# RWKV-7 and GLA trunk on one core: the recurrence's right sides and state update moved to ScalarE and one PSUM bank

## The chip, the core and the metric

The kernel runs on one core of one Trainium2 chip. The time of a run is the device time of that core in microseconds (us). TensorE is called PE, VectorE DVE, ScalarE ACT, GpSimd POOL, and SP is the queue that issues the loads. PSUM is the memory that PE writes to; it has eight banks.

## What is computed

Two layers on 272 tokens of width 2048, each followed by a squared-ReLU MLP. The change concerns the first mixer, RWKV-7, whose core is a recurrence over tokens for each of 32 heads of 64 channels:

```python
def step(S, inp):
    r_t, w_t, k_t, v_t, a_t, b_t = inp
    sa = einsum('bhvk,bhk->bhv', S, a_t)
    S = S * w_t[:, :, None, :] + sa[..., None] * b_t[:, :, None, :] + v_t[..., None] * k_t[:, :, None, :]
    y = einsum('bhvk,bhk->bhv', S, r_t)
    return S, y
...
mu = mean(y); var = mean((y - mu)^2)
y = (y - mu) * rsqrt(var + eps) * ln_w + ln_b
out = ((y + bonus) * g) @ w_o
```

The second mixer (gated linear attention), the two MLPs and the norms are touched by nothing but the names of two PSUM tags.

## The kernel before

All weights are float32. `wload` brings one block of 128x1024 in by DMA, ACT rounds it to `hi` (L134), DVE computes the rest `lo` (L135), and `mm3` forms each product by three matmuls, hi by x-high, hi by x-low, lo by x-high (L140 to L142). `raw` has three buffers and `hi` and `lo` two each, so a block can be rounded only when PE has finished with the block before the last.

**The recurrence in chunks.** The 32 heads are worked off in four groups (g = 0 to 3) of eight heads, the tokens in four chunks (c = 0 to 3) of 64 and one (c = 4) of 16. For a group and chunk these pieces follow each other:

- `centre` (L553) brings the values, less their mean over a head, to the token layout (tile `uv`, copied by ACT, L564). `keys` (L566) transposes the keys (tile `bkt`, one buffer, ACT L571).
- `inner` (L574) multiplies the masked scores `AM` with the values (bank `pm`), and ACT takes the result out negated as the right side `rs` (L581).
- `state` (L584) multiplies `AR` with the state `S` (tile `sb`, 128 x 4 x 64): once into the bank `pu`, which DVE then adds to `rs` (L595, two instructions), and once into `pry`, the output's bank.
- `solve` (L598) multiplies `rs` with the inverted score matrix, and ACT copies the result into `uv` (L607).
- `emit` (L609) first forms the state's increment in `pu` (L616). DVE adds the old state and multiplies with the decays `WC`, two instructions of 128x256 (tile `S`, under L268, the line of the helper `tt`). Then it adds the output products (L624) and ACT copies the output (`yc`, L627).
- `turn` (L629) transposes the output of the chunk before into `hres`; `norm(g)` (L640) is a generator with two steps for each of a group's four feature blocks: a product for the variance (L648, bank `pm`), logarithm and exponential on ACT (L649, L650), then on DVE a scaling and an addition (L652, L268), the gate's products (L657, bank `pm`) and DVE's final product (L658).

**The inversion of the next group.** `scores(g+1, c)` (L407) forms the next group's score matrices (PE L416; DVE masks them: `AM`, `AMr`). When the last of the five stands, `invert(g+1)` (L423) solves all their triangular 32x32 systems side by side on DVE: transposes in (L431, L434), 30 steps of two dependent instructions (`upd`, `sysA`), transposes out (L445, L449). `merge(g+1)` (L523) puts the 32-blocks together: a transpose on DVE (L526) of the short chunk's part from `sysA` into an `rs` buffer, from which ACT copies it (L527), and PE products (L535, L545).

**What sets the order.** PE's order in this part is written out by hand (`manual_schedule`, from L756): beside the recurrence PE works through `products()`, the big projections, one step of three matmuls at a time. `R(n)` runs n steps, `until(n)` runs up to step n, with the counts in `GAPS` and `MARK`. `some(last, n)` runs n steps of the norm of the group before, `some(inv, 9)` writes out nine steps of the inversion. The orders of DVE and ACT are not written by hand: a scheduler decides them when the program is built, and each engine then works its own list strictly from front to back. A `wload` stands in the program at the fourth step of the block before.

Of the kernel before, what the change touches and what calls it, by code (L numbers as in the profile page):

```python
# [12 lines left out]
ALU = mybir.AluOpType  # L13
# [4 lines left out]
P = 128  # L18
# [4 lines left out]
T = NMETA + SEQ  # L23
# [3 lines left out]
HEAD = 64  # L27
# [26 lines left out]
class Kern:  # L54
# [24 lines left out]
        return self.pt("pj", 2)  # L79

    def pm(self):
        return self.pt("pm", 2)

    def ptr(self):
        return self.pt("pt", 2)
# [2 lines left out]
        return self.pt("pry", 1)  # L88

    def pu(self):  # L90
        return self.pt("pu", 1)

    def vec(self, name, j):
        c = VI[name] * KT + j
# [171 lines left out]
    def rwkv(self, done):  # L266
        nc, tc, ap = self.nc, self.tc, self.ap
# [67 lines left out]
        nc.vector.tensor_scalar(out=om0, in0=self.vecs[:, c : c + KT], scalar1=-1.0, scalar2=1.0, op0=ALU.mult,  # L335
                                op1=ALU.add)
        xr = [self.t(self.xp, [P, 2, T], "x", KT, F32R) for _ in range(KT)]
        pss = [f()[:, :T] for f in (self.pj, self.pj, self.ptr, self.ptr, self.pm, self.pm, self.pry, self.pu)]
        for kt in range(KT):
            nc.vector.scalar_tensor_tensor(out=hnp[:, kt, 1:], in0=d[:, kt], scalar=self.vec("norm_mix0", kt),  # L340
                                           in1=rstd, op0=ALU.mult, op1=ALU.mult)
# [22 lines left out]
        def lora(f):  # L364
            l2 = self.t(e2, [96, 2, P], "l2", 2)
            nc.sync.dma_start(l2, ap["lora2"][f])
            st = self.t(ep, [P, 2, T], "ca", 2)
            zw, za = self.pm(), self.pm()
# [83 lines left out]
        for f in range(KT):  # L452
# [26 lines left out]
            rk = self.pm()[:, :T]  # L479
# [32 lines left out]
        uvs, rss, bkts, rys, ys = {}, {}, {}, {}, {}  # L512

        def geom(g, c):
            full = c < NC4
# [57 lines left out]

        def inner(g, c):  # L574
            full, n, nr, am, lo, up, at = geom(g, c)
            uv, rv = uvs[g, c], half(self.pm())
            for h in range(8):
                nc.tensor.matmul(rv[at[h % 2][0], h // 2], am[:n, h, :n], uv[:n, h], start=True, stop=True)
            rs = rss[g, c] = self.t(kp, [P, 512], "rs", 2).rearrange("p (h v) -> p h v", h=8)
            for q in range(2):  # L580
                nc.scalar.mul(rs[up, q::2], rv[at[q][0]], -1.0)  # L581


        def state(g, c):  # L584
            full, n, nr, am, lo, up, at = geom(g, c)
            rs, AR = rss[g, c], ARs[g % 2]
            ry = rys[g, c] = half(self.pry())
            ra = half(self.pu())
            for p in range(4):
                for q, i in ((0, 0), (1, 1), (1, 0), (0, 1)):  # L590
                    rows = slice(64 * q, 64 * q + 64)
                    nc.tensor.matmul((ra, ry)[i][at[q][i], p], AR[rows, p, c * 128 + i * n : c * 128 + (i + 1) * n],
                                     sb[rows, p], start=i == 0 or p == 0, stop=i == 0)
            for q in range(2):
                nc.vector.scalar_tensor_tensor(out=rs[up, q::2], in0=ra[at[q][0]], scalar=-1.0, in1=rs[up, q::2],  # L595
                                               op0=ALU.mult, op1=ALU.add)

        def solve(g, c):  # L598
            full, n, nr, am, lo, up, at = geom(g, c)
            uv, rs, pu = uvs[g, c], rss[g, c], half(self.pu())  # L600
            nu = n if full else 16
            for h in range(8):
                o = n * (1 - h % 2)
                nc.tensor.matmul(pu[o : o + nu, h // 2], am[up, h, :nu], rs[up, h], start=True, stop=True)
            for q in range(2):
                o = n * (1 - q)
                nc.scalar.copy(uv[n : n + nu, q::2], pu[o : o + nu])  # L607

        def emit(g, c):  # L609
            full, n, nr, am, lo, up, at = geom(g, c)  # L610
            uv = uvs[g, c]
            if full:
                pS = half(self.pu())
                for h in range(8):
                    k = slice(64 * (h % 2), 64 * (h % 2) + 64)
                    nc.tensor.matmul(pS[k, h // 2], bkts[g, c][:, h // 2, k], uv[:, h], start=True, stop=True)  # L616
                src = pS
                if c:
                    tt(sb, pS, sb, ALU.add)
                    src = sb  # L620
                tt(sb, src, WC[:, 4 * g : 4 * g + 4, c : c + 1].to_broadcast([P, 4, HEAD]))
            ry = rys[g, c] if c else half(self.pry())
            for h in range(8):
                nc.tensor.matmul(ry[at[h % 2][1], h // 2], am[: 2 * n, h, n : 2 * n], uv[: 2 * n, h],  # L624
                                 start=c == 0 and h < 2, stop=h > 5)
            y = ys[g, c] = self.t(kp, [P, 4, HEAD], "yc", 2)
            nc.scalar.copy(y[: 2 * n], ry[: 2 * n])  # L627
# [120 lines left out]
        def some(it, n):  # L748
            for _ in range(n):
                next(it, None)  # L750
# [5 lines left out]
        with tc.manual_schedule(engines={mybir.EngineType.PE}):  # L756
# [9 lines left out]
            for g in range(NG):  # L766
                more = g + 1 < NG
                for c in range(5):
                    if c:
                        state(g, c)  # L770
                        turn(g, c - 1)
                    if more and c < 2:
                        scores(g + 1, 2 * c)
                    elif not more:
                        some(last, 1)
                    R(GAPS[g][c][0])
                    some(inv, 9)
                    solve(g, c)
                    if c in (1, 3):
                        centre(g, c + 1)  # L780
                    if c < 3:
                        keys(g, c + 1)
                    if more and c < 2:
                        scores(g + 1, 2 * c + 1)
                    some(last, 4)
                    R(GAPS[g][c][1])
                    if more and c == 1:
                        scores(g + 1, 4)
                        inv = invert(g + 1)
                    some(inv, 9)  # L790
                    emit(g, c)
                    if c < 4:
                        inner(g, c + 1)
                    if g + 2 < NG and c == 2:
                        fetch(g + 2, BKs, bkd)
                    if g + 2 < NG and c == 3:
                        fetch(g + 2, ARs, ard, 0, 512)
                    if g + 2 < NG and c == 4:
                        fetch(g + 2, ARs, ard, 512)
# [273 lines left out]
```

## Time and profile before

| | us |
|---|---|
| median of 3 runs | 2653.16 (2652.71 to 2655.34) |
| the profiled execution | 2651.93 |
| its span | 2649.9 |
| PE busy | 2551.9 (96%) |
| DVE busy | 1688.0 (64%) |
| ACT busy | 1257.3 (47%) |

The recurrence lies between about 325 and 665 us of the span. In the view of windows that stretch has PE busy for 291.08 of its 340 us, DVE for 235.25 and ACT for 155.55, at a mean granted PE clock of 0.94; from 700 us on PE is all but never idle. In a timeline a row's bracket tells the idle time of its engine before it and what ended it.

### The profile page before, as it was taken

To read this page: it belongs to the slowest core of one execution; us is meant where nothing else is said; L and a number is where in the kernel's file an instruction comes from. 1 tells how busy PE (TensorE), PEld (TensorE's weight loads), DVE (VectorE), ACT (ScalarE), POOL (GpSimd) and SP (SyncE) were. 2 spreads that over 40 slices of the span, in tenths; PEclk is the share of its full clock that TensorE was granted. 3 is DMA by queue.
4 is the path that set the end of the run, shared out by engine and by line. 5 is a ranking of instruction groups with operands and counts; after the bars stand their busy time and mean duration, and the time that the engine had idled before them with its cause. 6 is when DMAs were issued, how large, how long until landed. Compare 5 with 4: busy or idle time off the path is not lost.

```text
span 2649.9 us, 47706 instructions
## 1 busy us (share of the span) xinstructions
PE 2551.9 (96%) x19492; PEld 2364.2 (89%) x19492; DVE 1688.0 (64%) x2794; ACT 1257.3 (47%) x2011; POOL 10.8 (0%) x35
## 2 busy tenths in 40 slices
PE   7998988888999999999999999999999999999998
PEld 7887977777999999999999999998888888888887
DVE  8677976775755545545545666676766656656665
ACT  5364644445544434434434544454555535435444
POOL 0000000000000000000000000000000000000000
PEclk9998999989999999999999999999999999999999
DMA  5565732322455555555555544444555555555554
GB/s 192 180 217 205 245 137 85 100 79 93 160 174 176 175 175 175 176 176 178 177 177 176 176 150 148 155 167 144 188 186 189 186 189 189 186 189 189 186 190 159
DMA packets 137083, 450.17 MB, mean 170 GB/s; under 512 B 15760, under 2 KB 23696, under 8 KB 136864
## 3 DMA queue, kind: packets, MB, share of 16 engines
q1 hardware_dynamic: 136864, 447.12, 49.3%
q8 instruction: 153, 2.51, 0.4%
q14 instruction: 66, 0.54, 0.1%
HBM read 431.07 MB, written 15.99 MB: 169 GB/s over the span
## 4 chain that ended last, share of the span: by engine, by line
PE 77%; DVE 3%; ACT 1%; issue 0%; DVEq 0%; ACTq 0%
PE pj L168 23%; PE pj L140 13%; PE pj L142 13%; PE pj L141 13%; PE pj L169 12%; DVE lo L135 1%; PE pt L908 1%; PE pm L657 0%; PE pu L917 0%; DVE upd L268 0%; PE pt L897 0%; DVE sysA L268 0%; PE pm L648 0%; PE pm L558 0%; PE pt L416 0%
## 5 line engine op out<-in xcount | busy, mean ns | idle before, releaser
L134 ACT CAST hi<-raw 128x1024 fp32r<-128x1024 f32 (+1 forms) x834 | 813.6, 983 | 1086.7 <-PE pj L141 566.8
L135 DVE TENSOR_TENSOR lo<-raw,hi 128x1024 fp32r<-128x1024 f32 (+1 forms) x834 | 946.8, 1142 | 596.6 <-ACT hi L134 583.6
L140 PE MATMUL pj<-x,hi 128*128 128x272 f32 x2224 | 657.0, 296 | 6.6 <-ACT x L308 4.1
L142 PE MATMUL pj<-x,lo 128*128 128x272 f32 x2224 | 645.1, 290 | 0.2 <-DVE lo L135 0.2
L141 PE MATMUL pj<-x,hi 128*128 128x272 f32 x2224 | 643.4, 289 | 0.0
L168 PE MATMUL pj<-x,hi 128*128 128x512 f32 x1664 | 587.6, 396 | 0.6 <-DVE x L827 0.6
L169 PE MATMUL pj<-x,lo 128*128 128x256 f32 x1664 | 468.6, 282 | 1.3 <-DVE lo L135 1.3
L140 PEld LDWEIGHTS pj<-x,hi 128*128 128x128 f32 x2224 | 421.4, 190 | 15.1 <-ACT x L308 4.9
L141 PEld LDWEIGHTS pj<-x,hi 128*128 128x128 f32 x2224 | 424.2, 191 | 2.0
L142 PEld LDWEIGHTS pj<-x,lo 128*128 128x128 f32 x2224 | 420.7, 189 | 1.6 <-DVE lo L135 0.7
L168 PEld LDWEIGHTS pj<-x,hi 128*128 128x128 f32 x1664 | 313.2, 188 | 76.3 <-issue 2.9
L168 PE MATMUL pj<-h,hi 128*128 128x512 f32 x1024 | 358.5, 394 | 0.0
L169 PEld LDWEIGHTS pj<-x,lo 128*128 128x128 f32 x1664 | 314.1, 189 | 2.8 <-DVE lo L135 1.9
L140 PE MATMUL pj<-h,hi 128*128 128x272 f32 x1024 | 294.7, 288 | 0.0
L142 PE MATMUL pj<-h,lo 128*128 128x272 f32 x1024 | 293.9, 287 | 0.0
L141 PE MATMUL pj<-h,hi 128*128 128x272 f32 x1024 | 293.5, 287 | 0.0
L169 PE MATMUL pj<-h,lo 128*128 128x256 f32 x1024 | 288.5, 282 | 0.0
L168 PEld LDWEIGHTS pj<-h,hi 128*128 128x128 f32 x1024 | 192.4, 188 | 44.3
L141 PEld LDWEIGHTS pj<-h,hi 128*128 128x128 f32 x1024 | 193.7, 189 | 0.0
L169 PEld LDWEIGHTS pj<-h,lo 128*128 128x128 f32 x1024 | 193.5, 189 | 0.0
L140 PEld LDWEIGHTS pj<-h,hi 128*128 128x128 f32 x1024 | 192.6, 188 | 0.0
L142 PEld LDWEIGHTS pj<-h,lo 128*128 128x128 f32 x1024 | 192.1, 188 | 0.0
(246 smaller groups left out, 2223.1 us busy)
## 6 DMA issues: line engine op xcount, KB each, us to landing
raw<-mlp_w_d SPq DMA_DIRECT2D x512, 512.0 KB, 3.2
raw<-gla_in_d SPq DMA_DIRECT2D x98, 512.0 KB, 3.2
raw<-w_rkv_d SPq DMA_DIRECT2D x80, 512.0 KB, 3.7
raw<-gla_o_d SPq DMA_DIRECT2D x32, 512.0 KB, 3.2
raw<-w_r_d SPq DMA_DIRECT2D x16, 512.0 KB, 3.3
raw<-rw_oA_d SPq DMA_DIRECT2D x16, 512.0 KB, 3.3
raw<-rw_oB_d SPq DMA_DIRECT2D x16, 512.0 KB, 3.2
ard<-ar SPq DMA_DIRECT2D x16, 288.0 KB, 3.7
```

Of the source, the lines that this page charges most:

```text
L134: nc.scalar.copy(hi[:, h], raw[:, h])
L135: nc.vector.tensor_tensor(out=lo[:, h], in0=raw[:, h], in1=hi[:, h].bitcast(F32), op=ALU.subtract)
L140: nc.tensor.matmul(out, hi[:, ws], xh, start=first, stop=False)
L141: nc.tensor.matmul(out, hi[:, ws], xl, start=False, stop=False)
L142: nc.tensor.matmul(out, lo[:, ws], xh, start=False, stop=last)
L168: nc.tensor.matmul(wide, hi[:, ws], x[kt][:, :, off : off + SEQ], start=kt == 0, stop=False)
L169: nc.tensor.matmul(ps[:, :SEQ], lo[:, ws], x[kt][:, 0, off : off + SEQ], start=False, stop=kt == nk - 1)
L908: nc.tensor.matmul(pa[:w, i * C : (i + 1) * C], KX[i][:, dt, s * P : s * P + w], Q[:, dt, i * C : (i + 1) * C], start=dt == 0, stop=dt == 1)
```

## The change

- `inner` of the chunk c+1 writes into a `pu` bank and leaves it open; `state` adds its products with `S` into the same bank, so the sum of the right side forms in PSUM. A new function `sides` takes it out negated, two ACT instructions after `state`. DVE's two additions (L595) are gone.
- `carry` puts the old state into a further `pu` bank by four products with the identity matrix (c = 1 to 3). `learn` adds the increment to it there, and ACT writes the state in four instructions of 128x64, each scaled by a column of `WC`. DVE's addition and multiplication are gone.
- PSUM: `pu` has two banks, `pm` one (before one and two). Three other places take another tag for it (`rk`, `za`, one of eight accumulators).
- The hand-written order: `learn`, then `inner` of the next chunk, then `emit`, then `keys` of the next chunk (before: `keys` ahead of the increment, then increment, output, `inner`). The norm of the group before runs in chunks 2 and 3, two steps ahead of each gap; before it ran in chunks 0 and 1, four steps in a row. In the last group it stays where it was.

```diff
     def pm(self):
-        return self.pt("pm", 2)
+        return self.pt("pm", 1)
     def pu(self):
-        return self.pt("pu", 1)
+        return self.pt("pu", 2)
...
         def inner(g, c):
-            uv, rv = uvs[g, c], half(self.pm())
+            uv = uvs[g, c]
+            ra = ras[g, c] = half(self.pu())
             for h in range(8):
-                nc.tensor.matmul(rv[at[h % 2][0], h // 2], am[:n, h, :n], uv[:n, h], start=True, stop=True)
-            rs = rss[g, c] = self.t(kp, [P, 512], "rs", 2).rearrange("p (h v) -> p h v", h=8)
+                nc.tensor.matmul(ra[at[h % 2][0], h // 2], am[:n, h, :n], uv[:n, h], start=h < 2, stop=c == 0 and h > 5)
+            if c == 0:
+                sides(g, c)
+        def sides(g, c):
+            rs = ras[g, c, "rs"] = self.t(kp, [P, 512], "rs", 2).rearrange("p (h v) -> p h v", h=8)
             for q in range(2):
-                nc.scalar.mul(rs[up, q::2], rv[at[q][0]], -1.0)
+                nc.scalar.mul(rs[up, q::2], ras[g, c][at[q][0]], -1.0)
...
         def state(g, c):
-            for q in range(2):
-                nc.vector.scalar_tensor_tensor(out=rs[up, q::2], in0=ra[at[q][0]], scalar=-1.0, in1=rs[up, q::2],
-                                               op0=ALU.mult, op1=ALU.add)
+            sides(g, c)
...
+        def carry(g, c):
+            pS = pSs[g, c] = half(self.pu())
+            if c:
+                for p in range(4):
+                    nc.tensor.matmul(pS[:, p], self.ident, sb[:, p], start=p == 0, stop=False)
+        def learn(g, c):
+            uv, pS = uvs[g, c], pSs[g, c]
+            for h in range(8):
+                k = slice(64 * (h % 2), 64 * (h % 2) + 64)
+                nc.tensor.matmul(pS[k, h // 2], bkts[g, c][:, h // 2, k], uv[:, h], start=c == 0 and h < 2, stop=h > 5)
+            for p in range(4):
+                nc.scalar.mul(sb[:, p], pS[:, p], WC[:, 4 * g + p, c : c + 1])
         def emit(g, c):
-            if full:
-                pS = half(self.pu())
-                for h in range(8):
...
-                if c:
-                    tt(sb, pS, sb, ALU.add)
-                    src = sb
-                tt(sb, src, WC[:, 4 * g : 4 * g + 4, c : c + 1].to_broadcast([P, 4, HEAD]))
...
-                    elif not more:
-                        some(last, 1)
+                    some(last, 1 if not more else 2 if 1 < c < 4 else 0)
                     R(GAPS[g][c][0])
...
-                    if c < 3:
-                        keys(g, c + 1)
...
-                    some(last, 4)
+                    if c < 4:
+                        carry(g, c)
+                    some(last, 2 if more and 1 < c < 4 else 0 if more else 4)
                     R(GAPS[g][c][1])
...
+                    if c < 4:
+                        learn(g, c)
+                        inner(g, c + 1)
                     emit(g, c)
-                    if c < 4:
-                        inner(g, c + 1)
+                    if c < 3:
+                        keys(g, c + 1)
```

**What it moves in the engines' lists.** First PE, in group 1, chunk 1, between `solve` and the next `state`. In the old program, behind the `centre` product (L558), `keys` (L569) and pieces of the scores (L416), the norm of group 0 stands here, two feature blocks in a row (L648, L657), and then one step of the projections:

```order
L648 MATMUL pm_5111<-ysq_5109,cst_117 128x272
L657 MATMUL pm_5117<-gs_2_76,g_868_5107 128x272
L657 MATMUL pm_5117<-gs_3_77,g_868_5107 128x272
L648 MATMUL pm_5125<-ysq_5123,cst_117 128x272
L657 MATMUL pm_5131<-gs_2_76,g_872_5121 128x272
L657 MATMUL pm_5131<-gs_3_77,g_872_5121 128x272
L140 MATMUL pj_4911<-x_2114,hi_4810 128x272
```

In the new program the four identity products of `carry` (L617) stand between the scores and that step:

```order
L416 MATMUL pt_5069<-AR_433_2194,BK_432_2193 128x128
L416 MATMUL pt_5070<-AR_433_2194,BK_432_2193 128x128
L617 MATMUL pu_5081<-S_3523,cst_117 128x64 x4
L140 MATMUL pj_4920<-x_2114,hi_4819 128x272
L141 MATMUL pj_4920<-x_2114,hi_4819 128x272
L142 MATMUL pj_4920<-x_2114,lo_4820 128x272
```

The norm's six products are gone from here (they stand in chunks 2 and 3), `carry` is new, and `keys`, which stood ahead, now comes behind the output products.

Next DVE, near the end of the inversion that runs beside group 1. In the old program the transpose L526 stands in the middle of the steps, where `upd` has 210 columns, with DVE's state and right-side instructions around it:

```order
L268 TENSOR_TENSOR S_3523<-S_3523,WC_97 128x256
L268 TENSOR_TENSOR upd_5469<-sysA_2197 128x210
L526 STREAM_TRANSPOSE rs_5782<-sysA_2197 32x512
L268 TENSOR_TENSOR sysA_2197<-sysA_2197,upd_5469 128x10x21
L268 TENSOR_TENSOR upd_5472<-sysA_2197 128x198
L595 SCALAR_TENSOR_TENSOR rs_5591<-pu_5596,rs_5591 32x4x64
```

In the new program the last step (`upd_5573`), the four transposes out (L445) and the last two of L449 come ahead of it:

```order
L268 TENSOR_TENSOR upd_5573<-sysA_2197 128x30
L268 TENSOR_TENSOR sysA_2197<-sysA_2197,upd_5573 128x30
L445 STREAM_TRANSPOSE sysA_2197<-sysA_2197 32x8x32 x4
L449 STREAM_TRANSPOSE AM_434_2195<-sysA_2197 32x8x32 x2
L526 STREAM_TRANSPOSE rs_5800<-sysA_2197 32x512
L135 TENSOR_TENSOR lo_5708<-raw_5705,hi_5707 128x512 x2
```

So L526 has moved behind the whole inversion. In group 0 it stands in the new list ahead of the addition that belongs to the step of 168 columns, in group 2 ahead of the step of 84 columns; the split `lo` that comes next after it stands at the step of 58 columns in both.

Last ACT at the end of the same group: `yc` and `rs` of chunk 4, the copy L527 that reads what L526 wrote, `turn`'s copy into `hres`, the rounding of the next two blocks (`hi`), a copy out of a projection (`pj`) and the solution copy of chunk 4 (`uv`). In the old program:

```order
L627 COPY yc_5580<-pry_5395 128x256
L581 ACTIVATE rs_5591<-pm_5582 32x4x64 x2
L527 COPY AMr_435_2196<-rs_5782 32x16x8
L637 COPY hres_72<-pt_5615 128x4x64
L134 CAST hi_5689<-raw_5687 128x512 x2
L687 COPY hres_72<-pj_5511 128x272
L607 COPY uv_5503<-pu_5670 16x4x64 x2
```

In the new program, with the four state instructions (L625) ahead:

```order
L625 ACTIVATE S_3523<-pu_5507,WC_97 128x64 x4
L635 COPY yc_5610<-pry_5382 128x256
L587 ACTIVATE rs_5630<-pu_5593 32x4x64 x2
L645 COPY hres_72<-pt_5633 128x4x64
L527 COPY AMr_435_2196<-rs_5800 32x16x8
L134 CAST hi_5707<-raw_5705 128x512 x2
L695 COPY hres_72<-pj_5531 128x272
L610 COPY uv_5504<-pu_5688 16x4x64 x2
```

The copy L527 keeps its place ahead of the rounding of the next block, while the transpose that it waits for has moved back in DVE's list.

More of the change, by code (lines that the diff above doesn't have):

```diff
@@ L337, in rwkv @@
         xr = [self.t(self.xp, [P, 2, T], "x", KT, F32R) for _ in range(KT)]
-        pss = [f()[:, :T] for f in (self.pj, self.pj, self.ptr, self.ptr, self.pm, self.pm, self.pry, self.pu)]
+        pss = [f()[:, :T] for f in (self.pj, self.pj, self.ptr, self.ptr, self.pm, self.pu, self.pry, self.pu)]
         for kt in range(KT):
@@ L367, in lora @@
             st = self.t(ep, [P, 2, T], "ca", 2)
-            zw, za = self.pm(), self.pm()
+            zw, za = self.pm(), self.pry()
             nc.tensor.matmul(zw[:, :T], l2[:, 0], tw[:96], start=True, stop=True)
@@ L478, in rwkv @@
             nc.sync.dma_start(ard[f], ar)
-            rk = self.pm()[:, :T]
+            rk = self.pu()[:, :T]
             nc.tensor.matmul(rk, self.bones, kn, start=True, stop=True)
@@ L511, in rwkv @@
         half = lambda x: x[:, :256].rearrange("p (h v) -> p h v", h=4)
-        uvs, rss, bkts, rys, ys = {}, {}, {}, {}, {}
+        uvs, ras, bkts, rys, ys, pSs = {}, {}, {}, {}, {}, {}
         def geom(g, c):
@@ L575, in inner @@
             full, n, nr, am, lo, up, at = geom(g, c)
-            uv, rv = uvs[g, c], half(self.pm())
+            uv = uvs[g, c]
+            ra = ras[g, c] = half(self.pu())
             for h in range(8):
-                nc.tensor.matmul(rv[at[h % 2][0], h // 2], am[:n, h, :n], uv[:n, h], start=True, stop=True)
-            rs = rss[g, c] = self.t(kp, [P, 512], "rs", 2).rearrange("p (h v) -> p h v", h=8)
+                nc.tensor.matmul(ra[at[h % 2][0], h // 2], am[:n, h, :n], uv[:n, h], start=h < 2, stop=c == 0 and h > 5)
+            if c == 0:
+                sides(g, c)
+        def sides(g, c):
+            full, n, nr, am, lo, up, at = geom(g, c)
+            rs = ras[g, c, "rs"] = self.t(kp, [P, 512], "rs", 2).rearrange("p (h v) -> p h v", h=8)
             for q in range(2):
-                nc.scalar.mul(rs[up, q::2], rv[at[q][0]], -1.0)
+                nc.scalar.mul(rs[up, q::2], ras[g, c][at[q][0]], -1.0)
         def state(g, c):
             full, n, nr, am, lo, up, at = geom(g, c)
-            rs, AR = rss[g, c], ARs[g % 2]
+            AR, ra = ARs[g % 2], ras[g, c]
             ry = rys[g, c] = half(self.pry())
-            ra = half(self.pu())
             for p in range(4):
@@ L592, in state @@
                     nc.tensor.matmul((ra, ry)[i][at[q][i], p], AR[rows, p, c * 128 + i * n : c * 128 + (i + 1) * n],
-                                     sb[rows, p], start=i == 0 or p == 0, stop=i == 0)
-            for q in range(2):
-                nc.vector.scalar_tensor_tensor(out=rs[up, q::2], in0=ra[at[q][0]], scalar=-1.0, in1=rs[up, q::2],
-                                               op0=ALU.mult, op1=ALU.add)
+                                     sb[rows, p], start=i == 1 and p == 0, stop=i == 0 and p == 3)
+            sides(g, c)
         def solve(g, c):
             full, n, nr, am, lo, up, at = geom(g, c)
-            uv, rs, pu = uvs[g, c], rss[g, c], half(self.pu())
+            uv, rs, pu = uvs[g, c], ras[g, c, "rs"], half(self.pu())
             nu = n if full else 16
@@ L611, in emit @@
             uv = uvs[g, c]
-            if full:
-                pS = half(self.pu())
-                for h in range(8):
-                    k = slice(64 * (h % 2), 64 * (h % 2) + 64)
-                    nc.tensor.matmul(pS[k, h // 2], bkts[g, c][:, h // 2, k], uv[:, h], start=True, stop=True)
-                src = pS
-                if c:
-                    tt(sb, pS, sb, ALU.add)
-                    src = sb
-                tt(sb, src, WC[:, 4 * g : 4 * g + 4, c : c + 1].to_broadcast([P, 4, HEAD]))
             ry = rys[g, c] if c else half(self.pry())
```

## Prediction

> **What bounds the kernel now.** I read the page's first part, then the window of the recurrence, then who waits for whom on PE there. Span and window (us; busy time and count of each engine, granted PE clock, DMA share, GB/s):
>
> ```profile
> span 2649.9 us, 47706 instructions
> 325.00:665.00 340.00, 291.08 (x4081) 259.17 (x4081) 235.25 (x526) 155.55 (x356) 5.40 (x10) 0.94 0.31 102
> ```
>
> PE is busy for 291 of 340 us, so about 49 us of PE's time is idle in the only part that the change touches. PE's waits in this window (total us, times, longest):
>
> ```profile
> PE pu L592 <- DVE S L268: 17.8, 10, 3.3
> PE pm L648 <- DVE hres L658: 8.1, 6, 2.4
> PE pt L535 <- DVE sysA L445: 6.5, 2, 6.3
> ...
> PE pu L592 <- DVE upd L268: 5.0, 1, 5.0
> ```
>
> 22.8 us go to the new state S, which DVE makes late, 8.1 and more to the norm, 6.5 to the inversion. That is not yet what the removal is worth: DVE is full exactly where S is late. So I cut the recurrence into strokes, by the timeline of PE (the first `merge` product of each group, L535) and of DVE (the mask of the short chunk, AMr, after which the inversion runs, and its last transposes, L445). Start, length, line:
>
> ```profile
> 331.81 1.20 PE L535 MATMUL pt<-sysA,AM 32*32 32x32 f32 x64
> 408.78 1.20 PE L535 MATMUL pt<-sysA,AM 32*32 32x32 f32 x64
> 494.18 1.20 PE L535 MATMUL pt<-sysA,AM 32*32 32x32 f32 x64 [0.19 <-DVE sysA L445]
> 581.85 1.92 PE L535 MATMUL pt<-sysA,AM 32*32 32x32 f32 x64 [6.32 <-DVE sysA L445]
> ```
>
> ```profile
> 359.50 0.75 DVE L268 TENSOR_TENSOR AMr<-pt,cst 64x256 f32<-64x256 f32 x2
> 405.98 1.22 DVE L445 STREAM_TRANSPOSE sysA<-sysA 32x256 f32<-32x256 f32 x2
> 448.62 0.75 DVE L268 TENSOR_TENSOR AMr<-pt,cst 64x256 f32<-64x256 f32 x2 [0.96 <-PE pt L416]
> 534.04 0.75 DVE L268 TENSOR_TENSOR AMr<-pt,cst 64x256 f32<-64x256 f32 x2 [0.96 <-PE pt L416]
> ```
>
> From merge to mask, the **fronts**: 27.7 us in group 0, 39.8 in group 1, 39.9 in group 2. From mask to the next merge, the **tails**: 49.3, 45.6, 47.8. In two tails PE waits at the end for L445; in group 0 L445 ends at 407.2, 1.6 us before PE comes. So the tails are the inversion's length on DVE, and PE's waits for S inside them are mostly time that it would have waited at their end.
>
> **The change, part by part.** *The fronts.* Group 0 runs the same pieces as groups 1 and 2 but has no norm before it, so its front is the row for a front without one. The norm's move out of chunks 0 and 1 makes the other two like it. To that come three edits, with their rows: the wait for `centre`, the four `keys` transposes, and in the second mixer 32 matmuls of the identity product's form:
>
> ```profile
> 340.56 0.49 PE L558 MATMUL pm<-cst,hres 128*128 128x128 f32 x2 [0.84 <-ACT hres L687]
> 342.32 0.68 PE L578 MATMUL pm<-uv,AM 64*64 64x64 f32 x16 [0.84 <-ACT uv L564]
> 354.79 0.60 PE L569 MATMUL pm<-cst,BK 128*128 128x128 f32 x4
> 1546.40 3.56 PE L908 MATMUL pt<-Q,KX 128*128 128x64 f32 x32
> ```
>
> `carry`: four products are eight matmuls at 3.56/32 = 0.11 us, 0.85 us for each of 12; one lies in a front. `keys` of chunk 2 moves into the tail, -0.6. With one `pm` bank the first `keys` must wait until ACT has copied `centre` out; before it ran during `inner`'s wait of 0.84, now it follows: +0.6. Front 0 becomes 28.5 (+0.85). Fronts 1 and 2 lack the 0.84 that group 0 waits for `hres`, and run two projection steps less but one `turn` more, which I take as even: 27.7 each, -12.1 and -12.2. All fronts: **-23.4 us**.
>
> *S and the right side on ACT.* DVE's instructions that go, the norm's that come into the tails, the splits, and five transposes that follow the mask in group 0 (busy us, mean ns, idle before):
>
> ```profile
> L135 DVE TENSOR_TENSOR lo<-raw,hi 128x512 fp32r<-128x512 f32 x86 | 55.5, 687 | 24.3 <-ACT hi L134 23.6
> L595 DVE SCALAR_TENSOR_TENSOR rs<-pu,rs 64x256 f32<-64x256 f32 (+1 forms) x32 | 13.5, 421 | 8.6 <-PE pu L592 7.6 <-PE pj L141 0.2
> L652 DVE SCALAR_TENSOR_TENSOR ysq<-hres,vecs,ysq 128x272 f32<-128x272 f32 x16 | 8.0, 502 | 14.6 <-ACT ysq L650 14.4
> L658 DVE SCALAR_TENSOR_TENSOR hres<-r,vecs,pm 128x272 f32<-128x272 f32 x16 | 8.0, 497 | 3.0 <-PE pm L657 1.7
> L268 DVE TENSOR_TENSOR r<-r,ysq 128x272 f32<-128x272 f32 x16 | 7.1, 442 | 0.5
> ...
> L268 DVE TENSOR_TENSOR S<-pu,S 128x256 f32<-128x256 f32 x12 | 5.1, 423 | 0.9 <-PE pu L616 0.6
> L268 DVE TENSOR_TENSOR S<-S,WC 128x256 f32<-128x256 f32 x12 | 5.1, 422 | 0.2
> ```
>
> ```profile
> 360.28 2.67 DVE L431 STREAM_TRANSPOSE sysA<-AM 32x256 f32<-32x256 f32 x5
> ```
>
> Each tail loses six of L595 and six on S at 0.42: 5.1 us of DVE. Tails 1 and 2 gain four norm blocks of 0.50 + 0.44 + 0.50 = 5.8, and, as their fronts no longer leave DVE time for it, the five L431 behind the mask, 2.7. ACT takes S out of PSUM in four pieces; the nearest row is a copy of the same 128x64:
>
> ```profile
> 412.31 0.21 ACT L637 COPY hres<-pt 128x64 f32<-128x64 f32 x1
> ```
>
> So 0.84 for S on ACT, as long as DVE's two instructions, but the first `state` product needs only the first piece, and `inner`, output and `keys` (0.6 each) lie between `learn` and `state`: I cost it at nothing. If ACT has two roundings of 0.62 ahead of it, up to 0.5 of the wait comes back each time. The Trainium skill's page "ScalarE: Activation LUTs", section "Rules for kernel authors", speaks against the move: it gives about 0.3 us per instruction plus 0.83 ns per element, by an estimate 1.4 us for the four pieces. By the row they take 0.84; by the page the sum would lose less than 1 us, since the cover is longer.
>
> *What is late next: the transpose L526.* It feeds ACT's copy L527, which stands in ACT's list ahead of the rounding of the next weight block. ACT in the trace does wait there, for DVE, with the rounding behind it. The chain, and the steps that DVE has between L526's new places and L445 (start, length; the last row is all roundings of the window):
>
> ```profile
> 393.42 0.70 DVE L526 STREAM_TRANSPOSE rs<-sysA 32x512 f32<-32x512 f32 x1
> 398.66 0.32 DVE L268 TENSOR_TENSOR upd<-sysA 128x150 f32<-128x150 f32 x1
> 401.95 0.24 DVE L268 TENSOR_TENSOR upd<-sysA 128x84 f32<-128x84 f32 x1
> 403.46 1.16 DVE L445 STREAM_TRANSPOSE sysA<-sysA 32x256 f32<-32x256 f32 x2
> 407.11 1.24 DVE L449 STREAM_TRANSPOSE AM<-sysA 32x256 f32<-32x256 f32 x2
> ```
>
> ```profile
> 394.15 0.41 ACT L527 COPY AMr<-rs 32x128 f32<-32x128 f32 x1 [3.43 <-DVE rs L526]
> L134 ACT CAST hi<-raw 128x512 fp32r<-128x512 f32 x84 | 47.9, 617 | 33.1 <-PE pj L141 24.0 <-issue 7.7 <-ACT rs L538 0.6
> ```
>
> ```profile
> 410.39 0.29 PE L140 MATMUL pj<-x,hi 128*128 128x272 f32 x1
> 410.77 0.29 PE L140 MATMUL pj<-x,hi 128*128 128x272 f32 x1
> ```
>
> Before, L526 ran 14 us ahead of L445's end. In the new list PE can go no further than the block whose rounding precedes L527; 14 steps of 0.38 us, 5.3 us, and the output (0.6) still lie between there and the merge. PE, which no longer waits for S, gets there first and stands until L526 has run, the copy, a rounding and a split later. It restarts at a lower clock: after the 5.0 us wait above the granted clock was
>
> ```profile
> 365.00:370.00 5.00, 4.74 (x63) 4.65 (x64) 3.99 (x15) 1.51 (x3) 0.00 (x0) 0.59 0.01 3
> ```
>
> (its first figure is the window's length, 0.59 the clock). Some 4 us at half speed cost about 2 us after each stand. The tails then, each from the mask:
>
> - Tail 0: DVE 47.7 - 5.1 = 42.6 to L445's end; L526 ends 7.6 earlier (a step, 4.8 from 398.66 to 403.46, 2.4 for L445), at 35.0. The next split comes 2.9 later, after the step of 58 columns, and takes 0.7; steps and output 5.9, clock 1.8: 46.3, **-3.0**.
> - Tail 1: 45.4 - 5.1 + 5.8 + 2.7, less two splits of blocks and one addition that now come later (3.2): 45.6; L449 and L526 come after it, 47.5. Copy 0.4, two half roundings 1.2 and three copies of at most 0.4 before the output can run: 2.9; output 0.6, 12 steps 4.5, clock 2.0: 57.5, **+11.9**.
> - Tail 2: 47.7 - 5.1 + 5.8 + 2.7 - 3.6 (two splits, two additions): 47.5. Behind L526 stand three short steps, an addition, a split and L445, 5.6, so it ends at 41.9. Split done 2.2 later, steps and output 5.9, clock 2.0: 52.0, **+4.2**.
>
> Together **+13.1 us**. With L526 where PE never meets it, DVE alone would end the tails: 42.6, 45.6, 47.5 and about 1 more for PE's own added work. That is the other bound, -6; a DVE that also stands idle is the upper one, below.
>
> *The last group* has no inversion. Its waits for S (window 596 to 640):
>
> ```profile
> PE pu L592 <- DVE S L268: 4.1, 4, 1.2
> ```
>
> These go, 0.5 left for ACT's list; three `carry` 2.55 and `keys` 0.6 come, and its merge no longer runs at the lower clock, 0.8: **-1.3**. The other places that take another PSUM tag keep a bank each and have a projection between two uses: nothing, and less than 1 us if not.
>
> **Sum.** -23.4 + 13.1 - 1.3 = -11.6 us. Span 2649.9 to 2638.3; with the 2.0 us that the profiled execution (2651.93) has outside it, 2640.3; the median of the runs (2653.16) is 1.2 above that execution: 2641.5 us. By the uncertainty of clock, restart and DVE's gaps, some 2 us in each of five strokes, this case lies between 2634 and 2648.
>
> **Rivals.** *A: L526 holds nobody up.* If DVE keeps up with PE, the tails take 6 us less instead of 13 more: about 2623. For it: in group 0 PE reaches the place only shortly before L526. Against: DVE's windows are full in the tails, and the order puts L526 behind the whole inversion of group 1.
>
> *B: DVE stops at the norm.* In the tails the norm's first DVE instruction stands in the full list and waits for PE, then ACT's logarithm and exponential. Before, L652 waited 14.4 us over 16 times, 0.9 each, when nothing was behind it; now the inversion is. At 0.9 for eight blocks the tails grow by 7: 2649, no change. At 2.4, the longest wait of the norm on PE, by 19: 2661, slower. It decides at 1.5 each, and from 2.1 on the kernel is measurably slower. Against: by the lists PE's product stands some 4 us behind the mask, and DVE has transposes and nine short instructions, about 7 us, before it needs the result.
>
> *C: the change does not do what it says*, S waits in ACT's list instead of DVE's. Only the last group pays, 3.6: 2645.
>
> **How the numbers follow.** A measurement of this kernel can tell about 0.2%, 5.3 us, from no change. Forecast 0.53, A 0.09, C 0.06: together 0.68 faster (the edge of the forecast's range at no change is small enough to leave). B mild 0.17: same. B hard 0.15: slower. Range: forecast, C and mild B, 0.76, and the nearer half of A: 2624 to 2653.
>
> **What would show it.** In the new profile the strokes: fronts 28, 28, 28; tails 46, 57, 52. ACT's L527 waits for L526 for several us in each tail, PE's matmul L140 waits for ACT or DVE `hi`, `lo` in chunk 4, and PE's waits for S are under 2 us in all. Fronts near 40 or a PE wait at L535 for L445 instead would make it wrong; so would L660 (L652 of before) with idle time on DVE in the tails (rival B), or no wait at L527 (rival A).

## The result, and the profile after

| | before | changed |
|---|---|---|
| median of the runs side by side | 2652.71 us (2650.08 to 2655.34) | 2639.69 us (2634.79 to 2644.05) |
| ratio, 95% interval | | 0.9943 [0.9927, 0.9958] |
| profiled execution, its span | 2651.93, 2649.9 | 2640.85, 2639.1 |

The changed kernel is faster by 0.57%, 13 us of median, 11 us between the two profiled executions. 2641.5 us was forecast. One execution of the changed kernel in run 9, 2794 us at a granted clock of 0.845, is left out of the ratios.

First, who waits for whom on PE in the recurrence of the changed kernel (window 325 to 655; total us, times, longest):

```profile
PE pm L665 <- ACT ysq L657: 6.4, 10, 0.9
PE pm L569 <- ACT uv L564: 5.1, 4, 1.3
PE pj L140 <- ACT hi L134: 2.9, 3, 1.1
PE pj L142 <- DVE lo L135: 2.3, 2, 2.1
...
PE pu L597 <- ACT S L625: 1.2, 1, 1.2
```

The waits for S, 22.8 us before, are 1.2. None for the inversion's L445 is left: its last transpose is done 5.2, 9.9 and 5.4 us before the three merges, where the kernel before had 1.6, 0.1 and 0.1. In tail 1, whose merge starts at 491.20 us:

```profile
479.16 2.18 DVE L445 STREAM_TRANSPOSE sysA<-sysA 32x256 f32<-32x256 f32 x4
```

New are 5.1 us of waits at the keys (L569), and 5.2 at the rounding and the split of a weight block (L140, L142).

Then the strokes, by windows: front, tail, front, tail, front, tail (length; busy PE, PEld, DVE, ACT, POOL; last three: granted PE clock, DMA share, GB/s):

```profile
332.38:362.20 29.82, 27.29 (x467) 24.14 (x468) 10.67 (x19) 14.01 (x35) 0.95 (x1) 0.94 0.37 130
362.20:408.48 46.28, 43.17 (x557) 39.51 (x551) 42.86 (x102) 21.93 (x55) 0.68 (x2) 0.93 0.38 133
408.48:438.90 30.42, 28.74 (x477) 25.34 (x478) 9.63 (x18) 14.88 (x37) 0.95 (x1) 0.89 0.16 53
438.90:491.20 52.30, 47.52 (x581) 41.49 (x576) 46.93 (x114) 25.71 (x65) 0.68 (x2) 1.00 0.40 137
491.20:519.52 28.32, 26.32 (x477) 22.96 (x478) 9.63 (x17) 14.88 (x37) 0.95 (x1) 1.00 0.17 59
519.52:573.80 54.28, 48.17 (x557) 41.70 (x552) 48.30 (x121) 26.84 (x69) 0.68 (x2) 0.91 0.26 83
```

Fronts: 29.8, 30.4, 28.3. Tails: 46.3, 52.3, 54.3. The column to read first is PE's: it is busy in 47.5 of the 52.3 us of tail 1. In the kernel before, the same cut gave, for the three tails:

```profile
359.50:408.78 49.28, 39.75 (x529) 37.09 (x525) 46.28 (x112) 18.91 (x43) 0.68 (x2) 0.90 0.37 124
448.62:494.18 45.56, 40.41 (x556) 37.72 (x557) 42.38 (x105) 19.26 (x43) 0.68 (x2) 0.94 0.39 132
534.04:581.85 47.81, 37.24 (x533) 34.59 (x533) 44.91 (x115) 20.21 (x47) 0.68 (x2) 0.93 0.28 90
```

For the comparisons below each kernel's six strokes are added up. "PE idle" is their length less PE's busy time, "lost to the clock" the sum of length x (1 - granted clock); it is at most the loss, since a slow clock costs nothing while PE waits.

| us, from one profile each | six strokes | PE idle | lost to the clock |
|---|---|---|---|
| before | 250.0 | 40.5 | 15.8 |
| changed | 241.4 | 20.2 | 13.3 |
| changed, second profile (`e9_after_again`) | 240.9 | 20.7 | 12.0 |

20 us of idle time went, and the strokes are 8.6 shorter: 11.7 us came back as busy time of PE.

The two profiles of the changed kernel agree in the sum, but single strokes differ by up to 4.4 us (its first front took 34.2 us at a clock of 0.80). A difference of a few us in one stroke proves nothing. The whole time of one execution is no better guide. From the last norm product (the last L657, in the changed kernel L665) to the end, where the kernels differ in the names of PSUM tags at most, twelve of the fourteen profiles took 1987.5 to 1989.3 us, and those of runs 1 and 4 took 1999.7 and 1999.0.

### The profile page after: what moved, and what is told of

It is laid out like the page before. It is cut to its first block, busy times and chain, and to the rows that moved or that the text cites. A ratio compares the mean times of both kernels' runs of the same rounds, so it can differ in the third digit from the quotient of the medians.

```text
span 2639.1 us, 47851 instructions
## 1 busy us (share of the span) xinstructions
PE 2564.8 (97%) x19588; PEld 2373.6 (90%) x19588; DVE 1661.4 (63%) x2734; ACT 1271.9 (48%) x2075; POOL 10.8 (0%) x35
## 4 chain that ended last, share of the span: by engine, by line
PE 90%; DVE 5%; ACT 2%; DMA 2%; issue 1%; SPq 0%; DVEq 0%; ACTq 0%
PE pj L168 23%; PE pj L140 15%; PE pj L142 15%; PE pj L141 15%; PE pj L169 12%; DVE lo L135 1%; PE pt L416 1%; PE pj L195 1%; ACT hi L134 1%; PE pt L919 1%; DVE sysA L431 0%; PE pm L665 0%; DVE upd L268 0%; PE pm L558 0%; DVE sysA L268 0%
## 5 line engine op out<-in xcount | busy, mean ns | idle before, releaser
L140 PE MATMUL pj<-x,hi 128*128 128x272 f32 x2224 | 657.3, 296 | 9.6 <-ACT x L308 4.3
L142 PE MATMUL pj<-x,lo 128*128 128x272 f32 x2224 | 646.3, 291 | 2.9 <-DVE lo L135 2.8
L140 PEld LDWEIGHTS pj<-x,hi 128*128 128x128 f32 x2224 | 421.6, 190 | 17.9 <-ACT x L308 5.0
L142 PEld LDWEIGHTS pj<-x,lo 128*128 128x128 f32 x2224 | 421.3, 189 | 4.7 <-DVE lo L135 3.7
L140 PE MATMUL pj<-h,hi 128*128 128x272 f32 x1024 | 294.7, 288 | 0.0
L142 PE MATMUL pj<-h,lo 128*128 128x272 f32 x1024 | 293.9, 287 | 0.0
L140 PEld LDWEIGHTS pj<-h,hi 128*128 128x128 f32 x1024 | 192.6, 188 | 0.0
L142 PEld LDWEIGHTS pj<-h,lo 128*128 128x128 f32 x1024 | 192.1, 188 | 0.0
```

The source lines that it names most:

```text
L140: nc.tensor.matmul(out, hi[:, ws], xh, start=first, stop=False)
L142: nc.tensor.matmul(out, lo[:, ws], xh, start=False, stop=last)
```

## Experiments

Two theories went into them. **DVE sets the tails** is the prediction's: a tail lasts as long as DVE's inversion, PE's own work there is hidden, and ACT's copy L527, waiting for L526, holds the next weight block up. **PE sets the tails**, the rival formed from the profile after: PE's own products (the norm's, the identity products) make up what the waits left free. Ratios are to the kernel before, with 95% intervals.

**1. The norm alone.** The kernel before, with only the norm's place changed.

```diff
-                    elif not more:
-                        some(last, 1)
+                    some(last, 1 if not more else 2 if 1 < c < 4 else 0)
...
-                    some(last, 4)
+                    some(last, 2 if more and 1 < c < 4 else 0 if more else 4)
```

> The kernel before with one part of the change: the norm stands in chunks 2 and 3, S and the right side stay on DVE. Two theories. DVE sets the tails (the prediction's): fronts 1 and 2 fall from 39.8 and 39.9 to about 28 (-24), tails 1 and 2 get 5.8 us of norm and 2.7 of transposes on a full DVE (+17): about -7 us, ratio 0.997, with longer waits of PE for the inversion at L535. PE's own work sets the tails: DVE finds room in them, they grow only by the norm's products on PE (4 to 6 us each), and the change of the time is -12 to -16 us, ratio 0.995 or less, that is the whole gain without the chain. A third: the norm is worth nothing where it stands, ratio 1.000.

Measured: 0.9956 [0.9939, 0.9974]. The last four strokes, front 1 to tail 2:

```profile
408.86:436.06 27.20, 25.86 (x477) 22.68 (x476) 12.22 (x22) 13.89 (x33) 0.95 (x1) 1.00 0.18 61
436.06:492.49 56.43, 46.97 (x554) 42.32 (x549) 51.93 (x126) 23.36 (x53) 0.68 (x2) 0.91 0.38 126
492.49:519.70 27.21, 25.86 (x477) 22.69 (x476) 11.01 (x20) 13.89 (x33) 0.95 (x1) 1.00 0.18 62
519.70:573.56 53.86, 41.73 (x530) 37.20 (x526) 51.28 (x131) 24.08 (x57) 0.68 (x2) 0.94 0.26 85
```

Fronts -12.6 each, tails +10.9 and +6.1; all six strokes 243.2, -6.9. By the strokes this is the first theory's sum, but the sum alone does not show its cause: of the growth, 6.6 us in tail 1 and 4.5 in tail 2 are busy time of PE, 4.3 and 1.6 idle time, and PE waits for L445 at the end of tail 2 only (3.3 us). The ratio, -0.44%, lies between the two and excludes only "worth nothing". Most of the change's gain is this one move.

**2. The chain alone.** The changed kernel with the norm's two lines as before.

> The changed kernel with the norm back in chunks 0 and 1: the chain, the banks and the order of keys, output and state as changed. DVE sets the tails: each loses 5.1 us of DVE, but L526 blocks the next rounding, fronts get a carry and the wait of keys: 0 to +3 us against the kernel before, ratio 1.000 to 1.001. PE's own work sets the tails: 21 us of waits for S go, 11.3 us of carry products (12 of 0.94) and 5 us of waits at L569 come: -3 to -6 us, ratio 0.998 to 0.999. In both the waits of PE for S are under 2 us.

Measured: 0.9989 [0.9973, 1.0005], no difference that can be told, although PE has no wait for S left. The sum of the six strokes:

```profile
sum 241.93, PE 216.60 PEld 189.08 DVE 169.33 ACT 119.26 POOL 4.81; mean PE 36.10 PEld 31.51 DVE 28.22 ACT 19.88 POOL 0.80
```

PE's idle time fell from 40.5 to 25.3 us, and its busy time rose from 209.5 to 216.6. New in the idle time are 5.1 us at the keys in the whole window and 5.4 at the rounding and the split. The strokes are 8.1 us shorter than before, but they lost 6.8 us to the clock where the kernel before lost 15.8; and the last group took 82.6 us from merge to last norm product, at a clock of 0.92, against 78.8 at 0.96. So by the ratio the part that the change is named after gains almost nothing alone. The two parts, -0.44% and -0.11%, add up to the whole, -0.57%, as closely as their intervals tell.

**3. No identity products.** The increment alone is written as the new state.

```diff
-            if c:
-                for p in range(4):
-                    nc.tensor.matmul(pS[:, p], self.ident, sb[:, p], start=p == 0, stop=False)
...
-...uv[:, h], start=c == 0 and h < 2, stop=h > 5)
+...uv[:, h], start=h < 2, stop=h > 5)
```

> The changed kernel without the identity products: the old state is left out of the new one (S is only the newly learnt part, scaled). DVE sets the tails: the six carries in the tails were beside the inversion, only the three in fronts and the three of the last group count, -5 us against the changed kernel (ratio to the kernel before 0.9925). PE's own work sets the tails: all 12 count, 12 x 0.94 = -11 us (ratio 0.990).

Measured: 0.9926 [0.9900, 0.9953], strokes 234.6: -6.8 for the nine carries in them, of which the clock can be 3.3 (10.0 us lost against 13.3). The interval holds both expectations. The price of one carry is clear, and what it saves is not:

```profile
368.54 1.10 PE L617 MATMUL pu<-S,cst 128*128 128x64 f32 x8
369.45 0.37 PE L140 MATMUL pj<-x,hi 128*128 128x272 f32 x1
```

0.91 us from its start to that of the next product, here in the changed kernel; 0.85 was predicted (eight times the 0.111 of its row are 0.89).

**4. L527 away from ACT.** The copy behind L526 on POOL.

```diff
-            nc.scalar.copy(AMr[32:64, :, 0:16].rearrange("p h t -> p t h"), rg[:, :, 0:8])
+            nc.gpsimd.tensor_copy(AMr[32:64, :, 0:16].rearrange("p h t -> p t h"), rg[:, :, 0:8])
```

> The changed kernel with the copy behind the transpose L526 (L527) moved from ACT to POOL, so that no rounding of a weight block stands behind it. By the prediction's sum the block was worth about 15 us over three tails: -12 to -19 us against the changed kernel (ratio to the kernel before 0.987 to 0.990). PE's own work sets the tails: what goes is PE's waits for hi and lo, 5.2 us, and part of a stretch at half clock, together -4 to -8 us (0.991 to 0.993).

Measured: 0.9925 [0.9899, 0.9951], strokes 240.1 against 241.4 and 240.9. The strokes do not show the first theory's 12 to 19 us; the ratio is in the range of the second, with the near end of the first just inside its interval, and in run 12 the same edit brings nothing. What PE met at that block in the changed kernel (tail 0):

```profile
397.11 0.39 PE L140 MATMUL pj<-x,hi 128*128 128x272 f32 x1 [0.72 <-ACT hi L134]
...
399.77 0.59 PE L142 MATMUL pj<-x,lo 128*128 128x272 f32 x1 [2.14 <-DVE lo L135]
```

and with the copy on POOL (times shifted by some 4 us):

```profile
404.22 0.60 PE L142 MATMUL pj<-x,lo 128*128 128x272 f32 x1 [3.17 <-DVE lo L135]
```

The wait went from 2.86 to 3.17 us. ACT rounded earlier, but the split `lo` still stood in DVE's list behind the inversion's columns, which DVE worked through without a pause:

```profile
403.34 0.22 DVE L268 TENSOR_TENSOR upd<-sysA 128x58 f32<-128x58 f32 x1
403.48 1.29 DVE L135 TENSOR_TENSOR lo<-raw,hi 128x512 fp32r<-128x512 f32 x2
```

**5. One product per carry.** 256 columns at once.

```diff
-                for p in range(4):
-                    nc.tensor.matmul(pS[:, p], self.ident, sb[:, p], start=p == 0, stop=False)
+                nc.tensor.matmul(pS, self.ident, sb, start=True, stop=False)
```

> The changed kernel with each carry as one identity product of 256 columns instead of four of 64. Four took 0.94 us from start to next start; the nearest row of one product of about that width (L656, 272 columns) took 0.68. If PE's own work sets the time: 12 x 0.3 = -3.6 us against the changed kernel (ratio to the kernel before 0.993). If DVE sets the tails: half of that, -1.8 us (0.9936).

Measured: 0.9943 [0.9927, 0.9960], strokes 242.8: nothing. Yet the carry is cheaper than either theory had it:

```profile
367.99 0.70 PE L616 MATMUL pu<-S,cst 128*128 128x256 f32 x2
368.34 0.48 PE L140 MATMUL pj<-x,hi 128*128 128x272 f32 x1
```

0.35 us to the next start, 0.56 less than four took, 5.0 over the nine in the strokes. But the first front ran at a clock of 0.89 in this profile, and the strokes lost 14.9 us to the clock, against 13.3 and 12.0. One execution cannot show 5 us through that; the interval leaves room for 4.

**6. Keys in another bank.**

```diff
-            pb = self.pm()
+            pb = self.pm() if c else self.ptr()
```

> The changed kernel with the keys of chunk 0 in a bank of pt instead of the single bank of pm, so that they need not wait until ACT has copied centre out (5.1 us in four waits of 1.26). If these waits are on the path: -4 to -5 us against the changed kernel, and -3 more if the half clock of front 1 came from them (ratio to the kernel before 0.991 to 0.993). If PE only waits later instead (inner needs centre's copies too, and S's right side): 0 to -1 (0.994).

Measured: 0.9919 [0.9902, 0.9937], strokes 230.8, -10.6. Its first front, against the 29.8 us at 0.94 above (the other two took 27.1, at 1.00):

```profile
332.82:360.56 27.74, 26.14 (x467) 23.12 (x468) 10.69 (x20) 14.00 (x35) 0.95 (x1) 1.00 0.36 131
```

The waits themselves were 5.1 us in four places, three of them, 3.8 us, in the strokes. The rest goes with the clock: 3.3 us lost to it, against 13.3. In the changed kernel two waits stand close together at the head of front 0:

```profile
341.12 0.49 PE L558 MATMUL pm<-cst,hres 128*128 128x128 f32 x2 [0.84 <-ACT hres L695]
342.89 0.66 PE L569 MATMUL pm<-cst,BK 128*128 128x128 f32 x4 [1.28 <-ACT uv L564]
```

and the clock falls behind them, from 0.96 in the window from 340 to 345 us to 0.70 in the next:

```profile
345.00:350.00 5.00, 5.00 (x51) 4.19 (x51) 1.87 (x3) 0.75 (x3) 0.00 (x0) 0.70 0.01 4
```

In the second profile of the same kernel it falls to 0.50 for ten us, here the first five:

```profile
345.00:350.00 5.00, 5.00 (x44) 4.41 (x44) 1.29 (x2) 1.01 (x4) 0.00 (x0) 0.50 0.06 19
```

With only the first of the two waits left, the clock stayed at 1.00 in this run. Front 1 of the changed kernel has no wait but the keys' in this place, and the clock falls behind that too:

```profile
416.39 1.12 PE L569 MATMUL pm<-cst,BK 128*128 128x128 f32 x4 [1.26 <-ACT uv L564]
415.00:420.00 5.00, 3.74 (x28) 3.16 (x27) 0.00 (x0) 2.58 (x6) 0.00 (x0) 0.62 0.08 31
```

**7 and 8. Half an inversion**, in the changed kernel and in the one before.

```diff
-            for s in range(1, 31):
+            for s in range(1, 31, 2):
```

> The changed kernel with every second of the 30 columns of the inversion left out (the inverse is incomplete): about 9.9 us less of DVE in each of three tails. DVE sets the tails: each gets 4 to 8 us shorter, -12 to -24 us against the changed kernel (ratio to the kernel before 0.985 to 0.990). PE's own work sets them: only the waits at the rounding block go, 5.2 us, with some clock: -3 to -8 us (0.991 to 0.993).

> The kernel before with the same columns of the inversion left out. Here both theories hold DVE for what ends the tails: the 6.5 us at L535 go, and of the 22.8 us of waits for S, in which S stood in DVE's list behind the inversion, a part: -10 to -18 us, ratio 0.993 to 0.996. If DVE were not the limit in the tails of the kernel before either: -6 us or less (0.998).

Measured: 0.9915 [0.9893, 0.9937] and 1.0000 [0.9978, 1.0022]. The kernel before gains nothing from 7 to 8 us less of DVE in each tail. Its tails got no shorter, although the inversion's last L445 now ends 18 to 23 us before the merge:

```profile
358.39:409.89 51.50, 41.11 (x530) 38.44 (x525) 38.38 (x84) 18.92 (x43) 0.68 (x2) 0.87 0.35 119
450.29:498.88 48.59, 41.53 (x557) 38.89 (x557) 35.71 (x79) 19.16 (x43) 0.68 (x2) 0.89 0.39 128
538.05:585.68 47.63, 39.42 (x532) 36.74 (x532) 37.40 (x86) 20.12 (x47) 0.68 (x2) 0.85 0.24 79
```

DVE is busy in 38 of 51 us there, and PE is idle as long as before, 40.9 us in the six strokes against 40.5 (and loses 23.6 us to the clock against 15.8). The 6.5 us of waits at the merge are gone; those for S, 17.8 and 5.0 before, are 6.9 longer in all:

```profile
PE pu L592 <- DVE S L268: 24.7, 12, 4.5
PE pu L592 <- DVE upd L268: 5.0, 1, 5.0
```

The longest, and what DVE did meanwhile (S's addition stands in the list behind splits and transposes, not behind columns):

```profile
387.14 0.59 DVE L449 STREAM_TRANSPOSE AM<-sysA 32x256 f32<-32x256 f32 x1
387.76 1.29 DVE L135 TENSOR_TENSOR lo<-raw,hi 128x512 fp32r<-128x512 f32 x2
388.97 0.44 DVE L268 TENSOR_TENSOR r<-r,hres 128x272 f32<-128x272 f32 x1
389.42 0.60 DVE L449 STREAM_TRANSPOSE AM<-sysA 32x256 f32<-32x256 f32 x1
390.05 1.29 DVE L135 TENSOR_TENSOR lo<-raw,hi 128x512 fp32r<-128x512 f32 x2
391.38 0.42 DVE L268 TENSOR_TENSOR S<-pu,S 128x256 f32<-128x256 f32 x1
```

In each tail PE's busy time and its waits for S make up the length: 41.1 and 10.3 of 51.5 us, 41.5 and 7.1 of 48.6, 39.4 and 8.2 of 47.6. The scheduler wrote DVE's list anew for this kernel, so the run shows that the inversion's length is not the limit; it does not show that S would have waited as long in the old list.

In the changed kernel the shorter inversion gains 6 to 7 us by the ratios, within what was given for "PE sets them". The strokes, 229.1, are 12.3 shorter, the near end of the first theory's range, but up to 8.0 of that is the clock, and the last group took 3.3 longer at a lower clock (79.5 us from merge to last norm product, against 76.2). Tails: 41.3, 53.0, 48.3 instead of 46.3 (45.1 in the second profile), 52.3 (52.3), 54.3 (50.6). So tails 0 and 2 gain some us, and tail 1 does not move, though DVE has 8 us less in it.

**9 and 10. The changed kernel again, and S scaled by DVE**, in one instruction out of the bank that the carry has filled.

```diff
-            for p in range(4):
-                nc.scalar.mul(sb[:, p], pS[:, p], WC[:, 4 * g + p, c : c + 1])
+            tt(sb, pS, WC[:, 4 * g : 4 * g + 4, c : c + 1].to_broadcast([P, 4, HEAD]))
```

> The changed kernel as it is, beside the three others of this call: ratio to the kernel before 0.994, by every theory.

> The changed kernel with one part undone: DVE scales S out of its bank, in one multiplication of 0.42 us, in place of four pieces on ACT; the carry products stay, DVE still has half of its old work on S. If PE's waits for S came from the places of S's instructions in DVE's list, behind the splits of the weight blocks: they come back, 10 to 18 us in all, and the ratio to the kernel before rises to 0.997 to 1.000. If they came from the two instructions' own length: one of 0.42 us is shorter than ACT's four pieces, PE waits 1 us at most in all, ratio 0.993 to 0.994.

Measured: 0.9936 [0.9913, 0.9959] and 0.9961 [0.9939, 0.9983]. The waits come back:

```profile
PE pu L597 <- DVE S L268: 13.6, 6, 3.1
```

and the place in the list makes them: at 365 us S stands behind five transposes that follow the mask and one more, and DVE works them off without a pause while PE waits 3.09 us. Each tail has one wait at this place. Tails 0 and 1 have one more each, 2.0 and 1.8 us, where S stands behind steps of the inversion and a split.

```profile
361.74 2.69 DVE L431 STREAM_TRANSPOSE sysA<-AM 32x256 f32<-32x256 f32 x5
364.46 0.60 DVE L434 STREAM_TRANSPOSE sysA<-AMr 32x256 f32<-32x256 f32 x1
365.09 0.42 DVE L268 TENSOR_TENSOR S<-pu,WC 128x256 f32<-128x256 f32 x1
```

That is the first reading, though the ratio falls between the two forecasts. In time the 12.4 us of waits come out as 3 us in the strokes (244.0 against 240.9), because other waits of PE went: those for a block's rounding and split (4.1 us in the second profile of the changed kernel) and for `yc` (2.1) are not in this one. The ratios give 6.6 us, and their intervals overlap; the other 3.0 are in the last group, at a clock of 0.96 (79.2 us from merge to last norm product, against 76.2 at 1.00).

**11. Keys and gate in `pt`.** Run 6, with the norm's second product too.

```diff
-                pg = self.pm()[:, :T]
+                pg = self.ptr()[:, :T]
```

> The changed kernel with the keys of chunk 0 in a bank of pt (as in the run that did this alone, 0.9919) and the norm's second product (L665) there as well, so that it need not wait for the logarithm of the first (6.4 us in ten waits). If a wait of PE costs its own length: 0.9895 (2629 to 2626 us where the kernel before takes 2653). If it costs that and a stretch at half clock: 0.988. If these waits only move to the next product: 0.992.

Measured: 0.9872 [0.9842, 0.9902], median 2624.89 us, strokes 228.5. This version beats both kernels. In tail 1 the waits at L665 (2.6 us) went, and at the split, where the changed kernel had waited 0.21 us, PE now waits 3.6 (the last figure; total, times, longest):

```profile
PE pj L142 <- DVE lo L135: 5.7, 2, 3.6
```

The tail is 51.6 us instead of 52.3. In tail 2 the inversion is the limit again: L445 ends at 561.10, 0.15 us before the merge. In the last group the norm's waits at L656 and L665 (2.7 us in all in run 6) are gone, and it takes 71.8 us from merge to last norm product, against 75.0 in run 6.

**12. All four edits.** Runs 4 and 5 on top of it.

> The kernel of the run before this with two more edits: the copy behind L526 on POOL, and each carry as one product of 256 columns. By the runs that made these edits alone (-4.8 us and nothing, each uncertain by 6): 0.987 to 0.990. If the copy's gain was not real: 0.989 to 0.990, as the kernel without it.

Measured: 0.9872 [0.9843, 0.9901], strokes 229.4: no more than without them.

## Why the prediction came out right, point by point

The total held (2641.5 forecast, 2639.69 measured; profiled span -10.8 against -11.6). That it held so closely is in part luck: the fronts gained 4.6 us less than forecast, and the tails grew 2.9 less and the last group gained 1.4 more, so that the errors cancel. One of the prediction's reasons was wrong.

- **Fronts**: -23.4 predicted, -18.8 measured. The mechanism is shown by run 1: the norm's move takes 12.6 us from each, against 12.1 and 12.2. At full clock a front of the changed kernel takes 28.3, against 27.7 predicted: the keys wait 1.28, which I had put at 0.6, and `scores` 0.4 for a bank of `pt` (L416), which I had not seen. The other 1.5 and 2.1 us are stretches at a lower clock.
- **S leaves DVE's list**: right. 22.8 became 1.2, under the 2 named, and run 10 brings the waits back by putting one instruction back. S on ACT costs PE 1.2 us in one wait, as good as the nothing it was costed at.
- **The four pieces on ACT**:

```profile
362.01 0.93 ACT L625 ACTIVATE S<-pu,WC 128x64 f32<-128x64 f32 x4 [2.67 <-PE pu L623]
```

0.93 us against 0.84 by the row of a copy. The Trainium skill's page "ScalarE: Activation LUTs", section "Rules for kernel authors", from which 1.4 was worked out, gives by an estimate 0.35 us for a single piece, near the mean of 313 ns in the groups of instructions; the four overlap, so the sum of singles is too much.
- **Tails**: +13.1 predicted, +10.2 measured, by strokes -3.0, +6.7, +6.5 against -3.0, +11.9, +4.2. **This is the step that failed**: "So the tails are the inversion's length on DVE, and PE's waits for S inside them are mostly time that it would have waited at their end." The inversion does end two of the three tails of the kernel before, but run 8 shows that its length does not set them: with half of the columns gone it is done some 20 us early, the tails stay, and as much waiting as leaves their end stands at S. In the changed kernel it ends no tail: it is done 5 to 10 us before each merge.
- **L526 and L527**: the chain is there as described, ACT waits for L526 for 6.0, 6.3 and 1.0 us (several us in two tails, not in all three). But PE's stand at that block, from which the prediction made most of the tails' growth, is 2.86, 1.21 and 1.14 us, and run 4 shows that the copy's place on ACT hardly matters: the split is as late in DVE's own list.
- **What filled the tails instead** is PE's own work, for which the tails' sum had no term; only the other bound had about 1 us for it. In tail 1 of the changed kernel (busy us, mean ns, idle before):

```profile
L665 PE MATMUL pm<-gs,g 128*128 128x272 f32 x16 | 4.7, 418 | 2.6 <-ACT ysq L657 2.6
L656 PE MATMUL pm<-ysq,cst 128*128 128x272 f32 x8 | 2.8, 432 | 0.0
...
L617 PE MATMUL pu<-S,cst 128*128 128x64 f32 x16 | 2.2, 281 | 0.0
```

and what it had in that tail before:

```profile
L592 PE MATMUL pu<-S,AR 64*64 64x64 f32 (+1 forms) x48 | 2.3, 237 | 5.0 <-DVE S L268 5.0
```

9.7 us of products and 2.6 of waits between them came in, where 5.0 us of waits for S went out: I had moved the norm with its DVE instructions and left its PE products uncosted. A growth of like size was forecast because DVE's new work, 8.5 us, which was costed, happens to be about as large. In tail 1 the two are level: with less on DVE (run 7) nothing moves, and with fewer waits on PE (run 11) DVE's split makes PE wait instead.
- **Rivals.** A's time is out: a kernel in which ACT does not wait at L527 (run 4) gains nothing like the 18 us between A and the forecast. Its ground, that L526 holds nobody up, came nearer to the truth than the forecast's: PE stands there for 5.2 us in all. B's wait did come, L660 stands 11.0 us in six times in the window, up to 4.7, 1.4 for each of the eight blocks and so just short of the 1.5 named; but PE never waits for L445, so it ends no tail. C is out, since the waits for S are 1.2.
- **The last group**: -2.7 from the last merge to the end, against -1.3. From the merge to the last norm product it is 76.2 us in both profiles of the changed kernel, against 78.8 before, at a clock of 0.96. In run 8, with the group of the kernel before but no wait at its merge, it is 75.7 at 1.00. So the gain goes with the clock behind that wait, costed at 0.8; that the removed waits for S gain anything here is not shown.

What stays open: what S's waits would have been in the old list of DVE with a shorter inversion (run 8 has a new list); how much of the carry's 11 us is hidden (runs 3 and 5 hold 0 as well as the whole of it), and how large the gate's part of run 11's gain is: the profiles give 2.3 us in the strokes and 3.2 in the last group, the ratios 12, with intervals that overlap.

## What to carry to other kernels

When a step is moved into a stretch that seems to belong to another engine, cost its instructions on every engine there, and test the claim "this engine sets the stretch" by halving that engine's work: in the kernel before this changed nothing, and in the changed one it gained 6 to 7 us. Where two engines are level, the place in an engine's list (S behind transposes, a split behind columns) makes the wait, and neither busy time nor one removed wait tells the gain. Look for the banks that a change gives up: giving two products a bank other than the single `pm` (run 11) brought a further 0.6%.

## What the runs showed of the hardware

Short waits can cost more than their length. Two gaps of PE, 0.84 and 1.28 us within 3 us, were followed by a granted clock of 0.70 over 5 us in one execution and of 0.50 over 10 us in another of the same kernel; one gap of 1.26 us was followed by 0.62 over 5 us. It is not certain each time: with the keys' wait, the six fronts of the two profiles ran at 0.94, 0.89, 1.00, 0.80, 1.00 and 0.89, and with runs 3, 4, 5, 7 and 10, which have that wait too, 13 of 21 fronts ran below 1.00. Without it (runs 6, 11, 12), eight of nine ran at 1.00 and one at 0.94. Why the same gap brings the clock down in one execution and not in the next these runs do not show. The Trainium skill's page "TensorE: Matmul & The Clock Gate", section "HAM oscillation", gives as the rule no PE-idle gaps of more than some 3.4 us; by these rows a gap of little more than a third of that can be enough. The first front took 29.8 and 34.2 us in two profiles of one kernel, so some 4 us in one stroke is about the limit of what a single profile can tell.
